# A decayed running sum behind a matmul: the last five lumps of output stored by one queue, whole

## The chip, the cores and the metric

The kernel runs on one core of a Trainium2 chip. The core has five engines that matter here: TensorE (PE: matmuls; its weight loads are listed apart as PEld), VectorE (DVE), ScalarE (ACT), GpSimd (POOL) and SyncE (SP), which computes nothing and issues transfers. Transfers between the chip's memory (HBM) and the on-chip memory (SBUF) are carried by 16 DMA engines that all queues of the core share. SyncE's queue appears in the profile as q1, GpSimd's as q0.

The metric is the device time of one execution in microseconds (us). A profile is one further execution, whose span runs from its first to its last instruction.

## The reference

```python
B, S, D = 16, 2048, 1024            # x: [B, S, D], w: [D, D], decay: [D], all float32
xw = x @ w
out[:, 0, :] = xw[:, 0, :]
for t in range(1, S):
    out[:, t, :] = decay[None, :] * out[:, t - 1, :] + xw[:, t, :]
```

So there is a matmul of 32,768 rows by 1024 x 1024, and behind it, for each of the 16 batches and each of the 1024 features, a recurrence over 2048 time steps. Input and output are 134 MB each.

## The kernel before, in words

**Tiling.** The rows are cut into 64 chunks of 512 time steps, and the chunks are taken in pairs (1024 time steps), except the last two, which are worked one at a time. A tile is 128 output features by the time steps of its pair or chunk. There are K = 8 tiles to a pair, so 31 x 8 + 2 x 8 = 264 tiles (the list `slots`). In the code `left` is the tile's number counted from the end: -264 to -1.

**The path of a tile.** The chunk of x is loaded by GpSimd's queue with a cast to bf16 (`load`), turned by VectorE in 32x32 blocks (L115) and copied into the order that the matmul wants (L123). TensorE makes the tile in PSUM (L131), features on the partitions and time along the row. The recurrence is then run by VectorE's scan: directly on PSUM (L221), or for "paired" tiles on every second time step with the square of the decay (L201), in which case ScalarE scales (L169, L183) and GpSimd adds (L196, L246) to make the other half. VectorE's transpose in 32x32 blocks (L258, in `back`) brings the result from features x time back to time x features, into an output tile `ot`. There are four output tiles, used in turn (L95).

**The stores.** R = 4 tiles in a row (4 x 128 features, half of the output's 1024 columns) share one output tile. This is a lump, and the class `Outlet` (L266) looks after it: when the fourth tile has been transposed, `store` (L274 on) issues the transfers. The 128 partitions of the output tile are four quarters of 32, and each quarter goes out by a store of its own, in the order 0, 2, 1, 3. A store writes 512-byte pieces: 32 partitions x 32 pieces (512 KB) for a pair of chunks, 32 x 16 (256 KB) for a single chunk. `Outlet` takes the queues that share the four stores (`queues`: the i-th store goes to the i-th queue in turn) and a number of pieces into which each store is cut along time (`pieces`).

**The order of the work.** The order of the instructions on each engine is written out by hand: the dictionary `agenda` lists for the first 34 tiles and the last 20 which step of which tile comes when, and every instruction is pinned to that order. A queue issues in that order too: a transfer whose data is not ready holds back everything behind it on the same engine. On GpSimd the adds stand in the same line as its store issues.

**The end.** The last four tiles (`left` -4 to -1) have no `Outlet`. Their results are turned by TensorE (L387) into four blocks of 128 time steps by 512 features, copied out of PSUM by ScalarE and VectorE in turn (L391), and stored by SyncE in four stores of 256 KB with 2 KB pieces (L393).

**What the edit touches.** For each group of four tiles the main loop makes an `Outlet` (L547). Two special cases are given there: for the four lumps whose first tile has `left` -24, -20, -16 and -12, the queues are SyncE's and GpSimd's, and for the lump with `left` -8 the stores are cut in two. All other lumps have the defaults, SyncE's queue and whole stores.

Of the kernel before, what the change touches and what calls it, by code (L numbers as in the profile page):

```python
# [25 lines left out]
def kernel(  # L26
# [26 lines left out]
    nc = tc.nc  # L53
# [12 lines left out]
    R = K // 2  # L66
# [9 lines left out]
    def ring(pool, name, count, shape, dtype=FP32):  # L76
        i = turns[name] = turns.get(name, -1) + 1
        return pool.tile(shape, dtype, name=f"{name}{i % count}")
# [46 lines left out]
    def matmul(ps, n, k, xt, t0=0, t1=TL, start=0, pairs=None):  # L125
        if pairs is None:
            rhs = xt[:, k // 2, k % 2, t0:t1]
        else:
            rhs = pairs[:, k // 2, t0 // P:t1 // P, :, k % 2].rearrange("p j i -> p (j i)")
        lhs = wsb[:, k, n].rearrange("p q i -> p (q i)")  # L130
        pin(nc.tensor.matmul(  # L131
            out=ps[:, t0:t1] if ps.shape[1] >= t1 else ps,
            lhsT=lhs,
            rhs=rhs,
            start=(k == 0 and t0 == start),
            stop=(k == K - 1),
        ))
# [376 lines left out]
    def usual(s):  # L514
        paired = [t.paired for t in tiles]
        do = [f"P{s}"] if paired[s] else []
        if paired[s - 1]:
            do.append(f"S{s - 1}")
        if not paired[s]:
            do.append(f"S{s}")  # L520
        do.append(f"C{s - 1}")
        if paired[s - 2]:
            do.append(f"B{s - 2}")
        if not paired[s - 1]:
            do.append(f"B{s - 1}")
        return do + later.get(s, []) + ["L"] * (2 if len(loads) > NQ else 1)

    def rest(s):
        do = [f"S{s - 1}"] if tiles[s - 1].paired else []
        do.append(f"C{s - 1}")  # L530
        if tiles[s - 2].paired:
            do.append(f"B{s - 2}")
        return do + [f"B{s - 1}"] + later.get(s, []) + ["L"] * len(loads)

    def perform(do):
        for deed in do:
            deeds[deed[0]](int(deed[1:] or 0))
# [3 lines left out]
    for step, (g, n) in enumerate(slots):  # L541
        T = TL * len(g)
        left = step - len(slots)
        if n % R == 0:
            ns, nj = range(n, n + R), T // P
            both = -6 * R <= left < -2 * R
            outlets = [Outlet(ns, nj, queues=(nc.sync, nc.gpsimd) if both else (nc.sync,),  # L547
                              pieces=2 if left == -2 * R else 1)]
        if left == -R:
            outlets = []  # L550
        if step == 0:
            heads = [ring(psp, "ps", 3, [128, T]) for _ in range(3)]
            firsts = [ps[:, 0:TL] for ps in heads] + [spares[0]]
            seconds = [ps[:, TL:T] for ps in heads] + [spares[1]]
            for j0, j1 in halves:
                for k in range(0, K, 2):
                    for i in range(R):
                        matmul(firsts[i], i, k, xt_of[0], j0 * P, j1 * P, pairs=xw_of[0])
            for k in range(1, K, 2):
                for i in range(R):  # L560
                    matmul(firsts[i], i, k, xt_of[0])
            for k0 in range(0, K, 2):
                for i in range(R):
                    for k in (k0, k0 + 1):
                        matmul(seconds[i], i, k, xt_of[1], 0, H * P,
                               pairs=xw_of[1] if k0 < 4 else None)
            for i in range(R):
                for k in range(K):
                    matmul(seconds[i], i, k, xt_of[1], H * P, TL, H * P,
                           pairs=xw_of[1] if i < 2 else None)  # L570
        if step < R:
            ps = heads[n] if n < 3 else tuple(spares)
        else:
            if step == K + 1:
                ps = nexts
            elif len(g) == 2 or n % R < 3:
                ps = ring(psp, "ps", 3, [128, T])
            else:
                ps = ring(psp, "spare", 1, [128, TL])
            todo = [(k, l) for k in range(K) for l in range(len(g))]  # L580
            if step < K:
                todo.sort(key=lambda kl: kl[0] % 2)
            elif step == K:
                todo = []
                nexts = ring(psp, "ps", 3, [128, T])
                for l in range(len(g)):
                    for i, both in enumerate((ps, nexts)):
                        for k in range(K):
                            matmul(both[:, l * TL:(l + 1) * TL], n + i, k, xt_of.get(g[l]),
                                   pairs=xw_of[g[l]] if g[l] in (3,) else None)  # L590
            elif step == K + 1:
                todo = []
            if left == -1:
                ps = tuple(both[:, t:t + TL // 2] for t, both in zip(
                    (0, TL // 2), (ps, ring(psp, "ps", 3, [128, TL]))))
                for t, half in zip((0, TL // 2), ps):
                    for k in range(K):
                        matmul(half, n, k, xt_of[g[0]], t, t + TL // 2, t)
                todo = []
            for k, l in todo:  # L600
                matmul(ps[:, l * TL:(l + 1) * TL], n, k, xt_of[g[l]])
        tiles.append(Tile(g, n, ps, outlets))
        do = agenda.get(step, agenda.get(left) if left >= -20 else None)
        if do is None:
            do = usual(step)
        else:
            do = do.split()
            if left == -20:
                do = rest(step) + do
        perform(do)  # L610
# [29 lines left out]
```

## Time and profile before

| what | value |
|---|---|
| runs | 908.35 us in the median of three (907.34, 908.35, 908.75) |
| profiled execution | span 907.2 us; the page gives no other time for it |
| TensorE busy | 892.8 us, 98% of the span |
| VectorE, ScalarE, GpSimd busy | 826.3, 686.2, 663.0 us |
| stores by SyncE's queue | 244 of 512 KB, 4 of 256 KB and 8 of 128 KB from `ot`, 4 of 256 KB at the end |
| stores by GpSimd's queue | 4 of 512 KB, 4 of 256 KB (5.7 us of GpSimd for the eight issues) |
| TensorE's granted clock | 0.998 of full speed |

How to read it. The time line gives, for each entry, the start and the duration in us from the start of the span, the engine (SPq is SyncE's queue), the line of the kernel, the operation, what it writes and reads, and how many were merged; in brackets stand the engine's idle time before it and what ended that. For a store, the duration is that of its issue only; the data moves afterwards, and "landing" is when the last of it has been confirmed. The table of stretches gives the length, then busy time and number of instructions of PE, PEld, DVE, ACT and POOL, then TensorE's granted clock, the mean busy share of the 16 DMA engines, and GB/s. The lines of queues give packets, MB and share of the 16 DMA engines.

### The profile page before, as it was taken

How to read it: one execution, taken by the hardware profiler on the slowest of the kernel's cores; microseconds unless marked ns; L12 is line 12 of the kernel's file. 1: busy time of each engine (PE TensorE's matmuls, PEld its weight loads, DVE VectorE, ACT ScalarE, POOL GpSimd, SP SyncE). 2: the span in 40 equal slices, each digit the busy share in tenths (PEclk: the TensorE clock that was granted, in tenths of full speed). 3: DMA queues.
4: the chain of work that ended last, by engine and by line, in shares of the span. 5: the costliest groups of instructions: out<-in, count | busy, mean ns of one | idle time of the engine just before them, and what ended most of it. 6: DMA issues, size and time to landing. Idle time of an engine off the chain costs nothing.

```text
span 907.2 us, 12004 instructions
## 1 busy us (share of the span) xinstructions
PE 892.8 (98%) x4119; PEld 411.4 (45%) x4201; DVE 826.3 (91%) x628; ACT 686.2 (76%) x955; POOL 663.0 (73%) x763
## 2 busy tenths in 40 slices
PE   9999999999999999999999999999999999999996
PEld 5444444444444444444444444444444444444443
DVE  4999989999999999899999999999999999999996
ACT  4889867777777877877877778778778778777742
POOL 7888678877777767768677777777677686776562
PEclk9999999999999999999999999999999999999999
DMA  9999999999999999999999999999999999999788
GB/s 194 194 215 220 227 215 220 215 238 255 249 250 254 241 243 259 247 244 228 227 233 227 227 232 227 226 232 233 220 230 231 228 231 223 232 229 207 153 161 211
DMA packets 397230, 204.77 MB, mean 226 GB/s; under 512 B 8816, under 2 KB 395376, under 8 KB 397168
## 3 DMA queue, kind: packets, MB, share of 16 engines
q1 hardware_dynamic: 258960, 131.62, 59.6%
q0 software_dynamic: 137920, 71.85, 58.1%
q8 instruction: 33, 0.54, 0.2%
q10 hardware_dynamic: 288, 0.52, 0.2%
q14 instruction: 29, 0.24, 0.1%
HBM read 138.42 MB, written 134.22 MB: 301 GB/s over the span
## 4 chain that ended last, share of the span: by engine, by line
PE 93%; DMA 2%; POOL 1%; issue 1%; DVE 1%; ACT 0%; POOLq 0%; DVEq 0%
PE ps L131 93%; DMA xb<-in_x_dram 2%; POOL ot L299 1%; POOL xb L105 1%; PE spare L131 1%; DVE xw L115 0%; ACT xt L123 0%; ACT xs L183 0%; DVE so L201 0%; PE spare L387 0%; DVE ot L258 0%; ACT h L169 0%; PE ps L387 0%; POOLq L635 0%; POOL xs L196 0%
## 5 line engine op out<-in xcount | busy, mean ns | idle before, releaser
L131 PE MATMUL ps<-xt,wsb 128*128 128x512 bf16 x3942 | 863.5, 378 | 4.7 <-ACT h L169 0.2
L131 PEld LDWEIGHTS <-wsb 128*128 128x128 bf16 x4152 | 405.9, 98 | 479.9 <-ACT wsb L306 0.8
L196 POOL TENSOR_TENSOR xs<-h,xs 128x512 f32<-128x512 f32 (+1 forms) x190 | 243.0, 1279 | 181.8 <-ACT h L169 79.4
L183 ACT COPY xs<-ps 128x1024 f32<-128x1024 f32 (+1 forms) x190 | 189.4, 997 | 155.3 <-PE ps L131 144.2
L258 DVE STREAM_TRANSPOSE ot<-so 128x1024 f32<-128x1024 f32 (+1 forms) x260 | 300.1, 1191 | 2.1 <-POOL so L190 1.1
L246 POOL TENSOR_TENSOR so<-h,xs 128x512 f32<-128x512 f32 (+1 forms) x190 | 241.4, 1272 | 39.0 <-ACT h L169 25.7
L123 ACT COPY xt<-xw 128x2048 bf16<-128x2048 bf16 (+1 forms) x136 | 242.3, 1790 | 7.8 <-DVE xw L115 7.6
L105 POOL DMA_DIRECT2D xb<-in_x_dram x264 | 174.3, 661 | 3.3 <-DMA ot<-in_w_dram 1.1
L169 ACT ACTIVATE h<-so,dec 128x512 f32<-128x512 f32 (+1 forms) x190 | 145.4, 766 | 27.7 <-DVE so L201 24.4
L115 DVE STREAM_TRANSPOSE xw<-xb 128x2048 f32<-128x2048 f32 (+1 forms) x78 | 147.4, 1901 | 5.5 <-DMA xb<-in_x_dram 5.5
L201 DVE TENSOR_TENSOR_SCAN so<-spare,keep,xs 128x512 f32<-128x512 f32 (+1 forms) x97 | 120.0, 1239 | 27.7 <-POOL xs L196 27.4
L201 DVE TENSOR_TENSOR_SCAN so<-spare,xs 128x512 f32<-128x512 f32 x93 | 113.3, 1220 | 27.6 <-POOL xs L196 24.6
L169 ACT ACTIVATE h<-ps,dec 128x512 f32<-128x512 f32 (+1 forms) x190 | 130.3, 686 | 0.0
L221 DVE TENSOR_TENSOR_SCAN so<-dec,ps 128x1024 f32<-128x1024 f32 x34 | 76.8, 2261 | 1.0 <-ACT h L169 1.0
L221 DVE TENSOR_TENSOR_SCAN so<-dec,keep,ps 128x1024 f32<-128x1024 f32 (+1 forms) x35 | 75.9, 2169 | 0.1
L250 ACT COPY keep<-so 128x1 f32<-128x1 f32 x136 | 25.3, 189 | 9.9 <-DVE so L221 9.4
L192 ACT COPY so<-keep 128x1 f32<-128x1 f32 x97 | 18.4, 191 | 2.6 <-DVE ot L258 2.4
L131 PE MATMUL ps<-xw,wsb 128*128 128x256 bf16 (+1 forms) x68 | 11.2, 301 | 0.1
L190 POOL MEMSET so<- 128x1 f32 x93 | 10.7, 117 | 0.6 <-DVE ot L258 0.6
L131 PE MATMUL spare<-xt,wsb 128*128 128x512 bf16 (+1 forms) x48 | 10.0, 335 | 0.0
L282 POOL DMA_DIRECT2D out_dram<-ot x8 | 5.7, 722 | 5.5 <-DVE ot L258 5.1
L299 POOL DMA_DIRECT2D ot<-in_w_dram x12 | 6.6, 546 | 3.3 <-DMA xb<-in_x_dram 2.0
(38 smaller groups left out, 44.5 us busy)
## 6 DMA issues: line engine op xcount, KB each, us to landing
out_dram<-ot SPq DMA_DIRECT2D x244, 512.0 KB, 10.9
xb<-in_x_dram POOLq DMA_DIRECT2D x248, 256.0 KB, 7.8
xb<-in_x_dram POOLq DMA_DIRECT2D x16, 128.0 KB, 5.8
out_dram<-ot POOLq DMA_DIRECT2D x4, 512.0 KB, 11.6
ot<-in_w_dram POOLq DMA_DIRECT2D x12, 128.0 KB, 5.1
out_dram<-ot SPq DMA_DIRECT2D x4, 256.0 KB
out_dram<-ot POOLq DMA_DIRECT2D x4, 256.0 KB, 8.5
out_dram<-ot SPq DMA_DIRECT2D x8, 128.0 KB, 4.3
```

The lines of the kernel that those rows point to most:

```text
L105: pin(nc.gpsimd.dma_start(out=xb_of[c][quad(q), j0:j1], in_=_ap(x, [[D, P], [P * D, j1 - j0], [1, CQ]], (b * S + t0 + j0 * P) * D + q * CQ)))
L115: pin(nc.vector.transpose(out=dst.rearrange("p (m j i) -> p j m i", m=M, i=P)[:, j0:j1, m0:m1], in_=src.rearrange("p (j m c) -> p j m c", ...
L123: pin(copy(out=xt_of[c][:, m0:m1, :, j0 * P:j1 * P], in_=src))
L131: pin(nc.tensor.matmul(out=ps[:, t0:t1] if ps.shape[1] >= t1 else ps, lhsT=lhs, rhs=rhs, start=(k == 0 and t0 == start), stop=(k == K - 1),))
L169: pin(nc.scalar.activation(out=h, in_=src, func=mybir.ActivationFunctionType.Copy, scale=dec[:, self.n:self.n + 1]))
L183: pin(nc.scalar.copy(out=self.xs, in_=self.ps))
L196: pin(nc.gpsimd.tensor_tensor(out=odds, in0=self.g, in1=odds, op=ALU.add))
L201: pin(nc.vector.tensor_tensor_scan(out=so[:, 3:T + 2:2], data0=squares[-1][:, n:n + 1].to_broadcast([128, T // 2]), data1=self.xs[:, 1:T:2 ...
L221: pin(nc.vector.tensor_tensor_scan(out=so[:, t + 2:t + 2 + size], data0=dec[:, n:n + 1].to_broadcast([128, size]), data1=ps, initial=befor ...
L246: pin(nc.gpsimd.tensor_tensor(out=self.so[:, 2:T + 2:2], in0=self.h, in1=self.xs[:, 0:T:2], op=ALU.add))
L250: pin(nc.scalar.copy(out=self.keep, in_=self.so[:, self.T + 1:self.T + 2]))
L258: pin(nc.vector.transpose(out=outlet.ot[:, :, c0:c0 + P], in_=self.so[:, 2 + t0:2 + t0 + nj * P].rearrange("p (i t) -> p i t", t=P)))
```

## The change

The two special cases are taken out. Every lump that has an `Outlet` is now stored by four whole stores on SyncE's queue.

```diff
         left = step - len(slots)
         if n % R == 0:
             ns, nj = range(n, n + R), T // P
-            both = -6 * R <= left < -2 * R
-            outlets = [Outlet(ns, nj, queues=(nc.sync, nc.gpsimd) if both else (nc.sync,),
-                              pieces=2 if left == -2 * R else 1)]
+            outlets = [Outlet(ns, nj)]
         if left == -R:
             outlets = []
```

For two lumps of 512 KB stores and two of 256 KB stores, GpSimd's queue had the second and the fourth store in the order 0, 2, 1, 3, that is quarters 2 and 3, and SyncE's had quarters 0 and 1. Now SyncE's has all four. The fifth lump, which was eight stores of 128 KB on SyncE's queue, is four of 256 KB. No instruction of TensorE, VectorE or ScalarE is added, removed or moved. GpSimd's program loses its eight store issues. SyncE's gains these eight and loses four, as the fifth lump's go from eight to four; all its stores keep their order.

## The prediction

> **What bounds the kernel now.** I read the page first, for the engine that the body hangs on:
>
> ```profile
> span 907.2 us, 12004 instructions
> PE 892.8 (98%) x4119; PEld 411.4 (45%) x4201; DVE 826.3 (91%) x628; ACT 686.2 (76%) x955; POOL 663.0 (73%) x763
> PE 93%; DMA 2%; POOL 1%; issue 1%; DVE 1%; ACT 0%; POOLq 0%; DVEq 0%
> ```
>
> TensorE is busy for 98% of the span, and its line makes 93% of the chain that ended last. The edit touches nothing before about 861 us, so only the last 46 us matter. There I followed the time line of SyncE's queue (start, duration, engine, line) together with the last copies of the other engines:
>
> ```profile
> 875.02 0.92 SPq L282 DMA_DIRECT2D out_dram<-ot  x2
> 893.73 0.32 SPq L282 DMA_DIRECT2D out_dram<-ot  x1
> 896.93 1.73 SPq L282 DMA_DIRECT2D out_dram<-ot  x1
> ...
> 897.73 0.59 ACT L391 COPY xb<-spare 128x512 f32<-128x512 f32 x1 [1.67 <-PE spare L387]
> 899.04 0.69 DVE L391 COPY h<-spare 128x512 f32<-128x512 f32 x1 [0.18 <-PE spare L387]
> ...
> 900.80 1.45 SPq L393 DMA_DIRECT2D out_dram<-xb  x3
> 902.66 0.33 SPq L393 DMA_DIRECT2D out_dram<-h  x1
> ```
>
> The first of the four final copies is done at 898.32, but its store is issued at 900.80: 2.5 us of waiting behind the eight stores of the fifth lump, which hold the queue from 893.73 to 900.70. The last copy is done at 899.73, its store leaves at 902.66, lands 3.3 us later at 906.0, and 1.2 us of closing work make the span of 907.2. So the end hangs on the stores, not on compute. Call the five lumps A (2.1 MB, first store 861.66), B (2.1 MB, 875.02), C, D and E (1.05 MB each, 880.96, 888.37, 893.73), and the last 1.05 MB, stored line by line at L393, V.
>
> Third, the table of stretches (length, busy time of each engine, clock, DMA share, GB/s):
>
> ```profile
> 849.00:852.00 3.00, 3.00 (x15) 1.37 (x14) 2.97 (x3) 1.95 (x5) 1.88 (x2) 1.00 0.97 171
> 852.00:855.00 3.00, 3.00 (x16) 1.37 (x14) 2.09 (x3) 3.00 (x5) 2.19 (x4) 1.00 1.01 217
> 855.00:858.00 3.00, 3.00 (x15) 1.37 (x14) 3.00 (x2) 1.83 (x3) 2.11 (x2) 1.00 1.02 242
> ...
> 876.00:879.00 3.00, 3.00 (x15) 1.36 (x14) 2.78 (x4) 1.76 (x7) 2.99 (x5) 1.00 0.83 160
> 879.00:882.00 3.00, 2.95 (x14) 1.36 (x14) 2.98 (x6) 1.97 (x8) 2.21 (x4) 1.00 0.83 168
> 882.00:885.00 3.00, 3.00 (x16) 1.37 (x14) 2.96 (x4) 1.09 (x5) 1.95 (x3) 1.00 1.01 207
> ...
> 898.00:900.00 2.00, 1.01 (x10) 0.77 (x8) 1.55 (x3) 0.91 (x2) 0.00 (x0) 1.00 0.55 113
> 902.00:905.00 3.00, 0.00 (x0) 0.00 (x0) 0.00 (x0) 0.00 (x0) 0.00 (x0) 0.87 0.96 357
> ```
>
> The first three rows are the lump before A, stored by SyncE alone in the row order 0, 2, 1, 3 of 32-partition quarters: it starts at 171 GB/s and reaches 242 once neighbouring stores overlap. In B, SyncE has quarters 0 and 1 only, and stays at 160 to 168. GpSimd's half of B was issued at 875.30 but moves only after SyncE's half:
>
> ```profile
> q1 hardware_dynamic: 1937, 0.98, 83.2%
> ...
> q0 software_dynamic: 285, 1.07, 90.5%
> q1 hardware_dynamic: 248, 0.12, 8.3%
> ```
>
> The first line is 876 to 882 us (q1 is SyncE's queue; packets, MB, share), the other two 882 to 888. So the two queues took turns here; they did not add up. At 898 to 900 the DMA engines are only 55% busy, at 113 GB/s, while SyncE issues E piece by piece.
>
> **The change part by part.** The profiled execution has no time on the page but its span, 907.2, which is 1.2 under the median of the three runs (908.35; they spread from 907.34 to 908.75). I work on the span and carry the difference over to the median.
>
> *Removed from GpSimd: eight store issues.* They cost 5.7 us of busy time and 5.5 us of idle time ahead of them. What is queued behind them are the adds of L196 and L246. VectorE has no wait on GpSimd after 864 us but one, of 0.22 us at 877.66, where the add stood behind B's issue. TensorE runs without a gap to 896.7. So this is worth 0 to 0.2 us; I take 0, since the last scans wait for TensorE's last columns. The rows that hide it are VectorE's, busy 5.00 us of 5 in nearly every stretch from 865 to 895.
>
> *Added to SyncE: the same eight stores, and four for E instead of eight.* Four issues of 512 KB took 5.8 us in the lump at 848.08 (0.32, 0.56, 2.14, 2.64), the later two held until earlier stores had drained. After the change A holds the queue to about 867.5, with B due at 875.02. B holds it to 880.8, and C is due at 880.96. C's four then enter as B drains, to about 885.5, before D is due at 888.37, and D's before E is due or shortly after. No lump waits long for the queue itself. E's four, at the prices of its first four now (0.32 + 1.78 + 0.97 + 1.73 and gaps, 4.98 us), would be through at 898.7, 0.4 us after V's first copy; if they find the queue drained, sooner. Freed: E's other four issues, 2.0 us, which today stand right ahead of V.
>
> *Moved: the bytes.* This is the sum. B starts moving at 875.85 (its packets begin about 0.8 us after the issue, as now), unless A is late: A alone on SyncE needs the 12.0 us of the lump at 834.27 (last landing 8.9 after its fourth issue at 837.41), so it lands at 873.7 against 875.7 now. B by the three rows above: 3 us at 171, 3 at 217, 3 at 242 is 1.89 MB, and the remaining 0.21 MB at 242 takes 0.9: drained at 885.7 (now 888). C follows without a gap and in the alternating order of quarters, so I take the warm row: 1.05 MB at 242 is 4.3 us, to 890.0. D is due before that: to 894.4. E's first packets come 0.85 after 893.73, at 894.6. Its drain is 4.3 us warm (898.9) and 4.9 us if it climbs through 171, 217 and 242 again (899.5); I take 899.5, since D has just run out. Today E drains at about 902.1, when the 2 KB packets of V take over. V's 1.05 MB at the 357 GB/s of 902 to 905 take 2.9 us: 902.4. V's last store is due at 899.73, issued by about 900.0, so it does not limit (2.6 us from issue to landing at the shortest: 902.6). From the last bytes to the landing now: 905.0 to 906.0, 1.0 us. So 903.4, and with the 1.2 us of closing 904.6: the gain is 2.6 us, 0.29%. From the median: 908.35 - 2.6 = 905.8.
>
> Nothing is newly waited for in the buffers: the four output tiles are reused in turn, so E writes over A, which lands at 873.7, long before.
>
> The page "SBUF — State Buffer" of the Trainium skill (section "Can I just issue two DMAs to hit both halves?") speaks against this: partitions 0 to 63 reach no more DMA ports than 0 to 31, and two DMAs on the two halves do not combine (it gives 6%). The first half of it the trace bears out: B's quarters 0 and 1 stay at 160 to 168 GB/s. The second it does not: the lump at 848 goes from 171 to 242, which is 42%. By that rule C to E would stay near the first rate, which is the first rival.
>
> **The rivals.**
>
> *One queue never leaves the slow rate (slower).* If stores of 512 packets in one queue keep to one half of the partitions at a time, B to E run at the 168 GB/s of 879 to 882: 5.25 MB take 31.3 us, to 907.1, then V 2.9 + 1.0 + 1.2: 912.2, 5.0 over, 913.3 in median. The point that decides is the mean rate over B to E: now it is 5.25 MB from 875.85 to 902.1, 200 GB/s; below that the kernel gets slower. At 185 it would be 910.5 in median. For it: the first 3 us of each lump. Against it: 217 and 242 right behind, in the same queue.
>
> *SyncE's issue becomes the bound (slower).* If E's four issues cost twice those of its half-sized pieces, 10 us from 893.73, V leaves at 903.7 instead of 900.80: 2.9 over, 911.3 in median. It decides from 900.7 on for E's last issue. For it: third and fourth issues of 2.1 to 2.6 us. Against it: those were twice as large, and were held by what was still to drain, and the queue at E's start holds only the end of D. The page "Perfetto Trace Analysis" of the Trainium skill (section "DMA Optimizations") has this as a rule: smaller pieces can start sooner, and where the making of descriptors limits, spreading over issuers may help. No row here separates the making of descriptors from the draining.
>
> *E starts into a drained queue and stays slow (no change).* D has drained by 894.4, so E may run all the way at the 168 to 171 of a lone store: 6.2 us, to 900.8, then V to 903.7, landing 904.7, span 905.9: gain 1.3, 907.1 in median. For it: the two SyncE stores of B never sped up. Against: they were neighbouring quarters, not alternating ones.
>
> **How the numbers follow.** A measurement of this kernel can tell about 0.2% (1.8 us) from no change; the three runs spread by 0.16%. Chances: the sum 0.55, of it 0.04 ending under 1.8 us of gain; the third rival 0.24; the slow rate 0.13; the issue 0.08. So faster 0.51, same 0.28, slower 0.21. The likeliest case has its own range: C to E at 260 GB/s would end with V's last store as the limit (902.6 + 1.2, 903.8; 904.9 in median), and at 217 GB/s C and D drain at 895.4, E at 900.2, V at 903.1, gain 1.9: 906.5. With the three runs' spread below, 904.6; the whole range reaches through the third rival and part of the slow ones, to 909.8.
>
> **What would show it.** Right: q1 alone carries bytes after 861 us; B drained by 886; rates of 217 GB/s or more from 879 to 894; V's first store issued within 0.6 us of 898.3; the last landing near 903.4. Wrong: a stretch from 882 to 894 under 200 GB/s (first rival), V's first store later than 900 with its copy long done (second), E alone at 170 GB/s between 895 and 901 (third). Also wrong would be a last copy later than 899.73, which I exclude since no compute instruction is moved.

## The result, and the profile after

The changed kernel takes 905.3 us in the median of five runs (905.08 to 905.47), against 908.35 for the kernel before. The ratio is 0.9966, with a 95% interval of 0.9954 to 0.9978: 0.34% faster, 3.0 us. The forecast was 905.8.

The page of the changed kernel says the same of the body as that of before. Only GpSimd's share has gone down, by the eight issues:

```profile
span 903.5 us, 11998 instructions
PE 892.3 (99%) x4119; PEld 411.1 (45%) x4201; DVE 825.5 (91%) x628; ACT 686.1 (76%) x955; POOL 657.2 (73%) x755
```

The span is 3.7 us shorter than that of before, as the pages round it. Of this, 0.4 us was there before the edit begins: the lump ahead of A, the same in both kernels, is issued at 847.64 instead of 848.08. What the edit did is the rest, 3.2 to 3.3 us. Where a time of the changed kernel is given "on the clock of before", these 0.44 us are added to it. The time line from E's first store on, to be laid beside the one in the prediction:

```profile
892.75 0.32 SPq L282 DMA_DIRECT2D out_dram<-ot  x1
...
897.05 0.59 ACT L391 COPY xb<-spare 128x512 f32<-128x512 f32 x1 [1.67 <-PE spare L387]
898.36 0.69 DVE L391 COPY h<-spare 128x512 f32<-128x512 f32 x1 [0.18 <-PE spare L387]
...
897.66 1.62 SPq L393 DMA_DIRECT2D out_dram<-xb  x3
899.39 0.39 SPq L393 DMA_DIRECT2D out_dram<-h  x1
```

The first final store leaves at 897.66, as soon as its copy is done (897.64); before, it stood 2.5 us behind the fifth lump. In the waits of SyncE's queue after 870 us this is to be seen as a new wait, now for ScalarE's copy and no longer for the queue (who waited for whom, us, times, longest):

```profile
SPq L393 <- ACT xb L391: 1.7, 1, 1.7
```

The table of stretches (last columns: clock, DMA share, GB/s) shows why the fifth lump was out of the way:

```profile
876.00:879.00 3.00, 3.00 (x15) 1.37 (x14) 3.00 (x5) 2.03 (x7) 1.78 (x3) 1.00 0.88 190
879.00:882.00 3.00, 2.95 (x14) 1.37 (x14) 2.97 (x5) 1.63 (x6) 0.94 (x3) 1.00 0.91 214
882.00:885.00 3.00, 3.00 (x16) 1.37 (x14) 3.00 (x5) 1.15 (x6) 1.37 (x2) 1.00 0.98 247
885.00:888.00 3.00, 3.00 (x16) 1.36 (x14) 3.00 (x6) 1.02 (x3) 1.47 (x2) 1.00 0.98 259
888.00:891.00 3.00, 2.95 (x15) 1.35 (x14) 3.00 (x4) 0.61 (x2) 0.74 (x1) 1.00 1.00 256
898.00:898.50 0.50, 0.33 (x3) 0.09 (x1) 0.32 (x2) 0.25 (x1) 0.00 (x0) 1.00 0.20 44
898.50:900.00 1.50, 0.00 (x0) 0.00 (x0) 0.56 (x1) 0.34 (x1) 0.00 (x0) 1.00 0.97 349
```

Two rows of before that the prediction does not show:

```profile
885.00:888.00 3.00, 3.00 (x16) 1.37 (x14) 3.00 (x5) 1.63 (x5) 1.33 (x2) 1.00 0.98 191
888.00:891.00 3.00, 2.95 (x15) 1.35 (x14) 3.00 (x5) 0.60 (x2) 2.12 (x4) 1.00 1.00 221
```

From 882 to 891 the one queue moves 247 to 259 GB/s, where the two queues moved 191 to 221. The stretch of 113 GB/s at 898 to 900 is gone: the mean there is now 273 GB/s, as V's stores move in it. The last two rows of the changed kernel split it up: E has all but drained at 898.0 (44 GB/s in the next half microsecond), before V's bytes begin at 898.5.

### The profile page after: what moved, and what is told of

Read it like the earlier page. It is cut to its first block, busy times and chain, and to the rows that moved or that the text cites. A ratio compares the mean times of both kernels' runs of the same rounds, so it can differ in the third digit from the quotient of the medians.

```text
span 903.5 us, 11998 instructions
## 1 busy us (share of the span) xinstructions
PE 892.3 (99%) x4119; PEld 411.1 (45%) x4201; DVE 825.5 (91%) x628; ACT 686.1 (76%) x955; POOL 657.2 (73%) x755
## 4 chain that ended last, share of the span: by engine, by line
PE 94%; DMA 1%; DVE 1%; issue 1%; POOL 1%; ACT 0%; DVEq 0%; POOLq 0%
PE ps L131 94%; DMA ot<-in_w_dram 1%; DMA xb<-in_x_dram 1%; PE spare L131 1%; POOL xb L105 1%; DVE so L221 1%; POOL ot L299 0%; DVE xw L115 0%; ACT xt L123 0%; DVE ot L258 0%; PE spare L387 0%; DVE so L201 0%; DVE wsb L306 0%; ACT xs L183 0%; PE ps L387 0%
## 5 line engine op out<-in xcount | busy, mean ns | idle before, releaser
L324 PE MATMUL spare<-idle 128*128 128x512 bf16 x22 | 6.9, 488 | 1.2 <-DVE idle L314 1.2
```

## The experiments

All ratios are to the kernel before, run on the same chip, where its median was between 908.35 and 908.92; the ratios are what compares.

| kernel | median us | ratio (95% interval) |
|---|---|---|
| changed kernel | 905.3 | 0.9966 (0.9954 to 0.9978) |
| one queue, fifth lump in pieces | 905.7 | 0.9963 (0.9950 to 0.9975) |
| two queues, fifth lump whole | 907.7 | 0.9986 (0.9977 to 0.9995) |
| one queue for A and B, fifth whole | 906.5 | 0.9978 (0.9969 to 0.9987) |
| one queue for C and D, fifth whole | 906.6 | 0.9975 (0.9964 to 0.9986) |
| one queue, neighbouring quarters | 909.2 | 1.0001 (0.9992 to 1.0010) |
| two queues, halves mixed | 907.4 | 0.9980 (0.9971 to 0.9989) |
| two queues, halves mixed, fifth whole | 906.1 | 0.9970 (0.9957 to 0.9982) |
| changed kernel, small GpSimd issues | 905.3 | 0.9961 (0.9949 to 0.9974) |
| changed kernel, fifth lump not stored | 905.8 | 0.9966 (0.9953 to 0.9978) |
| changed kernel, last store by ScalarE | 916.3 | 1.0084 (1.0070 to 1.0098) |

**Which half of the edit.** The first two kernels each make one part of it alone.

```diff
-            outlets = [Outlet(ns, nj)]
+            outlets = [Outlet(ns, nj, pieces=2 if left == -2 * R else 1)]
```

> Four lumps by SyncE's queue alone, the fifth still in eight pieces. Theory (the gain comes from bytes that drain faster when one queue takes the quarters in alternating order): the fifth lump's eight issues at 0.5 us each are through at about 897, before the first final copy at 897.6, so the time is that of the changed kernel, 3 us (0.33%) under before, within 0.6 us. Rival (the gain is that the fifth lump's issues no longer stand ahead of the final stores): the final stores leave near 900.8 as before, and the time is within 0.8 us of before.

```diff
-            outlets = [Outlet(ns, nj)]
+            both = -6 * R <= left < -2 * R
+            outlets = [Outlet(ns, nj, queues=(nc.sync, nc.gpsimd) if both else (nc.sync,))]
```

> Only the fifth lump is changed: whole stores, while the four lumps before it keep both queues. Theory (drain): the hole of 113 GB/s at 898 to 900 closes, but B to D still drain late; the fifth lump is drained at about 900.7 instead of 902.1, 1.4 us (0.15%) under before, about half of the change. Rival (issue): the whole gain of 3 us is here.

With one queue and the fifth lump still in eight pieces, the time is that of the changed kernel. The pieces cost nothing here, because the queue ahead of them is empty enough: they enter it at half a microsecond each and are through at 898.5, and the first final store, whose copy ends at 899.16, leaves at 899.18. (In the execution that was profiled everything stands 1.5 us later than in the changed kernel, from the lump ahead of A on, which is issued at 849.17.) With the fifth lump whole and two queues, a gain of 0.14% is left, as forecast: the hole at 898 to 900 closes to 209 GB/s, but the drain stays late. So the long issue of the pieces before was a consequence of the full queue, not its cause, and the pieces cost time only where the drain is late.

**Halves or queues.** This is the main question: is it that there were two queues, or which quarters each got? The third kernel keeps one queue and changes only the order of the quarters; the fourth keeps two queues and the pieces and deals the quarters otherwise.

```diff
-                for i, q in enumerate((0, 2, 1, 3)):
+                for i, q in enumerate(self.order):
...
-            outlets = [Outlet(ns, nj)]
+            late = -6 * R <= left
+            outlets = [Outlet(ns, nj, order=(0, 1, 2, 3) if late else (0, 2, 1, 3))]
```

> The changed kernel with the quarters of the last five lumps in the order 0, 1, 2, 3 instead of 0, 2, 1, 3. Theory (a store of 32 partitions uses half of what the DMA engines can read, and only neighbours from different halves add up): B to E drain at about 190 GB/s instead of 240, 27.6 us for 5.25 MB instead of 22, 5 us over the changed kernel and 2 over before (908 to 912 in all). Rival (the rate rises because more than two stores are in the queue, whatever their partitions): within 0.6 us of the changed kernel.

One queue with neighbouring quarters loses the whole gain: 909.2, level with the kernel before. Some of its stretches (the two left out have 201 and 193 GB/s):

```profile
876.00:879.00 3.00, 3.00 (x16) 1.35 (x14) 3.00 (x5) 2.21 (x8) 1.61 (x4) 1.00 0.85 176
879.00:882.00 3.00, 3.00 (x16) 1.35 (x15) 3.00 (x5) 1.44 (x7) 1.41 (x2) 1.00 0.86 173
...
888.00:891.00 3.00, 3.00 (x15) 1.34 (x14) 3.00 (x4) 0.61 (x2) 0.97 (x2) 1.00 0.95 230
```

Here the second store of B is of quarter 1 and brings nothing over the first. The right rows to lay beside these are those of a kernel with the order 0, 2, 1, 3 whose B starts at the same time. The changed kernel's B starts half a microsecond sooner (874.49 against 875.01); that of the kernel without E's stores, described further down, starts at 874.95:

```profile
876.00:879.00 3.00, 3.00 (x15) 1.37 (x14) 3.00 (x5) 2.22 (x8) 1.61 (x4) 1.00 0.85 176
879.00:882.00 3.00, 2.95 (x15) 1.37 (x14) 3.00 (x5) 1.45 (x7) 1.34 (x2) 1.00 0.93 218
```

So both start at 176 GB/s. In the next 3 us, as the second store follows the first, nothing is gained if it is quarter 1 (173), and 24% if it is quarter 2 (218). Taken by single microseconds, the order 0, 1, 2, 3 stays at 165 to 181 GB/s from 876 to 887 but for one: 245 from 882 to 883, which is where, at that rate, the bytes of quarter 1 end and those of 2 begin. From 888 on, with many stores of the smaller kind in the queue, it reaches 230 all the same. That is at least part of why the loss against the changed kernel was 0.35%, 3.2 us, and not the 5 expected.

```diff
             outlets = [Outlet(ns, nj, queues=(nc.sync, nc.gpsimd) if both else (nc.sync,),
-                              pieces=2 if left == -2 * R else 1)]
+                              pieces=2 if left == -2 * R else 1,
+                              order=(0, 1, 2, 3) if both else (0, 2, 1, 3))]
```

> The kernel before with the quarters of the four shared lumps dealt 0, 1, 2, 3, so that SyncE's queue gets quarters 0 and 2 and GpSimd's gets 1 and 3. Theory (halves): SyncE's part of A and B speeds up behind its first store from 168 towards 217 GB/s, its part of B takes 5.4 us instead of 6.2, and the end comes 0.8 to 2 us (0.1 to 0.2%) sooner than before. Rival (taking turns between two queues is itself the cost): within 0.5 us of before.

> The kernel before with quarters 0 and 2 on SyncE's queue and 1 and 3 on GpSimd's for the four shared lumps, and the fifth lump whole. Theory (what cost the time was that each queue's half came from one half of the partitions, not that there are two queues): the fifth lump is drained before 899.5 and the time is within 0.8 us of the changed kernel, 2.2 to 3 us under before. Rival (two queues take turns and lose by that): 1.3 us under before, as with the fifth lump whole alone.

The second of these is the same kernel without the line of `pieces`. Dealing the quarters so that each queue has one of either half brings 0.20% with two queues and pieces. With the fifth lump whole it brings 0.30%, and its interval covers the changed kernel's ratio. Two of its stretches, still with half of the four lumps' bytes on GpSimd's queue:

```profile
879.00:882.00 3.00, 2.95 (x14) 1.37 (x14) 3.00 (x5) 1.98 (x8) 2.28 (x4) 1.00 0.96 240
...
885.00:888.00 3.00, 3.00 (x15) 1.36 (x14) 3.00 (x5) 1.58 (x4) 1.39 (x2) 1.00 0.99 278
```

Before, these were 168 and 191. So most of what the two queues cost was not that there were two, but that each had its two stores from the same 64 partitions, while the queues' bytes went out one after the other. With the fifth lump whole, that is all that the runs can tell. With the pieces kept, two queues with mixed halves (0.9980) still stand behind one queue (0.9963); the intervals just touch. There the pieces are held again: the seventh takes 1.43 us to issue, at 897.47, and from 899 to 900 only 122 GB/s move.

**Which lumps.** With the fifth lump whole, one queue for one pair only: first for A and B, then for C and D.

```diff
-            both = -6 * R <= left < -2 * R
+            both = -4 * R <= left < -2 * R
```

> Fifth lump whole, the first two lumps (512 KB stores) by SyncE's queue alone, the third and fourth by both queues. Theory: most of the gain beyond the whole fifth lump is the second lump, drained at 885 instead of 888; 2 to 3 us under before. Rival (the third and fourth lumps, with their smaller stores, are what two queues slow): 1.3 us under before, as with the fifth lump whole alone.

```diff
-            both = -6 * R <= left < -2 * R
+            both = -6 * R <= left < -4 * R
```

> Fifth lump whole, the third and fourth lumps by SyncE's queue alone, the first two by both queues. Theory: the second lump is drained at 888 as before, the rest follows at about 245 GB/s, 3.15 MB in 12.9 us, to 901, as late as with the fifth lump whole alone: 1.0 to 2.0 us under before. Rival: the whole 3 us.

Both give about 2 us (0.22% and 0.25%), of which 0.14% is the whole fifth lump that both contain. What one queue adds to that is 0.08% for A and B and 0.11% for C and D, and with the 0.14% this makes 0.33%, about the changed kernel's 0.34%. The intervals, 0.1% to either side, are too wide to say whether the parts add up exactly. My view that most of it lay in the second lump falls. With B on two queues, C and D wait behind it in SyncE's queue, and then drain far faster than the 245 GB/s that I had put in, at 304 GB/s and in the next 3 us at 266:

```profile
888.00:891.00 3.00, 2.95 (x14) 1.37 (x14) 3.00 (x5) 0.60 (x2) 0.74 (x1) 1.00 1.08 304
```

**What bounds the end now.** The fifth lump's stores left out altogether:

```diff
-                if not outlet.missing:
+                if outlet.kept and not outlet.missing:
...
-            outlets = [Outlet(ns, nj)]
+            outlets = [Outlet(ns, nj, kept=left != -2 * R)]
```

> The changed kernel without the stores of the fifth lump, 1.05 MB that are left out of the output. Theory: in the changed kernel the fifth lump is drained at about 898.0, as the first final store's bytes begin to move, so the end now hangs on the final copies and issues, and the time falls by 0.5 us or less. Rival (the drain is still the bound): the time falls by 2 us or more, up to the 4 us that the 1.05 MB take.

Taking 1.05 MB of stores away saves nothing: 905.8, the ratio of the changed kernel. In its time line the final copies and stores stand to each other nearly as they did, all about 0.5 us later. The first and the last copy begin at 897.51 and 898.82, and their stores leave 0.61 and 1.24 us after that (0.61 and 1.03 in the changed kernel):

```profile
898.12 1.53 SPq L393 DMA_DIRECT2D out_dram<-xb  x3
900.06 0.33 SPq L393 DMA_DIRECT2D out_dram<-h  x1
```

So in the changed kernel the drain no longer sets the end; the final copies, their issues and their way to memory do.

**What GpSimd's freed time is worth.**

```diff
+                    if self.extra and i % 2:
+                        scrap = const.tile([128, 8], FP32, name="scrap", bufs=8)
+                        pin(nc.gpsimd.dma_start(
+                            out=scrap[quad(q)], in_=self.ot[quad(q), 0, c0:c0 + 8]))
```

> The changed kernel, with eight extra transfers of 1 KB from the output tile to a scrap tile issued by GpSimd at the places where its stores stood, so that GpSimd again waits for VectorE's transposes and spends its issue time. Theory: GpSimd's issues put off the fifth lump's first store by about 0.5 us against the first lump's (32.1 us between them in all kernels with these issues, 31.5 in the two without) and the last copy by 0.25 us, so the end moves by 0.2 to 0.5 us at most. Rival (a large part of the 3 us comes from the freed GpSimd): 1.5 us or more over the changed kernel.

Eight issues put back on GpSimd cost nothing that the runs can tell (905.3), and the 0.5 us by which E should have been late did not come (31.51 us from A's first store to E's). They are 0.5 us each instead of 0.65 to 0.8, and as they read only what the first tile of a lump wrote, they come sooner than the stores had: A's at 858.3, 3.5 us ahead of A's first store, where GpSimd's first store had come 0.3 us behind it. So this kernel does not bring back the delays that GpSimd's stores had made, and its test is weak. The kernel with mixed halves and the fifth lump whole says more: it has GpSimd's stores at their old places, and its time is the changed kernel's within the interval. A large share for GpSimd is out; the quarter of a microsecond that the traces show is not. From A's first store to the end of the last copy it is 38.07 us before and 38.05 with two queues for A and B, against 37.82 in the changed kernel, 37.82 with one queue for A and B, and 37.81 here. The two larger issues of B on GpSimd (875.30, 1.56 us) go with a wait of VectorE of 0.22 us at 877.66 that is gone in the changed kernel.

**A try for more.** As the end hung on the final stores' issue, the last one was given to ScalarE's queue.

```diff
-            pin(nc.sync.dma_start(
+            pin((nc.scalar if i == nb - 1 else nc.sync).dma_start(
                 out=_ap(out, [[D, 128], [1, CH]], (b * S + t0 + i * 128) * D + CH),
```

> The changed kernel with the last of the four final stores issued by ScalarE's queue, which is idle by then, instead of by SyncE's behind the third. Theory (the end now hangs on the final copies and their issues): the last store leaves at its copy's end, 0.3 us sooner, and so does the end: 0 to 0.4 us under the changed kernel, too little to be told apart by the runs. Rival (the drain still limits): no change in the last landing against the last copy.

It was 7.6 us slower than the kernel before, and so nearly 11 us slower than the changed one, for a reason that neither theory had. The waits of SyncE's queue and the time line name it:

```profile
SPq L282 <- DMA out_dram<-h: 13.2, 1, 13.2
...
886.34 15.75 SPq L282 DMA_DIRECT2D out_dram<-ot  x4
899.21 0.37 ACTq L393 DMA_DIRECT2D out_dram<-h  x1
```

SyncE's and ScalarE's transfers share eight completion semaphores, dealt out in turn when the program is built, and a store waits until the transfer that had its semaphore last has landed. The trace has the number of each transfer's semaphore: the last store got one ahead of a store of D. So D's second store, which stands long before it in the program, waited 13.2 us for that last store to land. The run says nothing on the 0.3 us that it was made for; no kernel here beats the changed one by more than its interval.

## Why the prediction was right, and which terms were off

*The end hangs on the drain of the stores (right for the kernel before).* The hidden cost was in the rate at which A to E leave, as the sum had it. The rate with alternating quarters was taken from the lump at 848 and held: 190, 214, 247 in B where the sum had 171, 217, 242, and 256 to 259 behind it instead of 242. One of the signs that it had named was missed by a hair: 214 GB/s from 879 to 882, where 217 was asked.

*E drained at 899.5 (mis-sized by about a microsecond).* It had all but drained at about 898.0, or 898.4 on the clock of before. About 0.5 us of it is that E was ready sooner against A's first store (31.52 us after it instead of 32.07), which the step on GpSimd's issues had put at nothing; the rest is the rate. The sum's 4.9 us for E's climb also hold only with steps half as long as those of the rows that it names, which it does not say; with their 3 us each it is 5.5.

*V follows at the drain's heels (did not hold).* The sum let V's bytes start as E's end and take 2.9 us. Once E was out of the way so early, V was bound by its own copies and issues, as leaving E out showed. Its bytes began half a microsecond after the drain. The last store was issued at 899.39, on the clock of before 899.8, and landed 3.2 us later, not in the 2.6 of the shortest. This is the path that the prediction had at the lower end of its range only, with V's last store as the limit; it put that at 904.9.

*The number.* On the clock of before the last landing was 903.1, against 903.4 in the sum. The closing took 0.9 us instead of 1.2; the traces of these kernels have either the one or the other, whatever the edit. So the gain in the median was 3.0 us where 2.6 were forecast. That the sum came so near owes something to luck: E was a microsecond early, and V did not follow it at once.

*GpSimd's issues are worth 0 to 0.2 us, taken as 0 (a little low).* The last copy comes 0.25 us sooner, and E's first store 0.55. The step had looked at VectorE's one wait of 0.22 us. The time lines show two more delays that are not listed as waits: before, VectorE's scan at 864.90 starts as the add behind A's issues ends (864.87), and its transposition at 879.03 as a later add ends (879.00). Counted from A's first store, VectorE was behind the changed kernel by 0.1 us at 874.92, 0.4 at 877.66 and 0.56 at 880.90. Of this, 0.25 us is left at the last copy: TensorE waited 0.22 us for GpSimd's add before its first final turning at 896.93, and in the changed kernel it does not.

*The first rival (one queue stays slow)* did not come, but its mechanism is real: the order 0, 1, 2, 3 brought it about, at 173 to 201 GB/s until 888, and cost the whole gain. The page "SBUF — State Buffer" of the Trainium skill says (section "Door 1: The DMA port swizzle (why `[64,N]` ≈ `[32,N]`)") that partitions 0 to 63 reach no more ports than 0 to 31. The trace agrees: 176 GB/s at first, then 173 as quarter 1 follows quarter 0. The same page says (section "Can I just issue two DMAs to hit both halves?") that two transfers, one from either half, measured only 6% over one. The traces do not agree: 218 GB/s once quarter 2 follows quarter 0, against 176 before, and 304 with a backlog of such stores. The measurement decides.

*The second rival (SyncE's issue)* did not come either: E's four issues took 3.2 us (892.75 to 895.93), not the 10 that it needed, and with the fifth lump in pieces, eight issues instead of four made no difference.

*The third rival (E cold and slow)*: E began in a nearly empty queue, as it said, but climbed within 2 us. By single microseconds from 893 on the rate was 173, 162, 242 and 288 GB/s; the rival needed the 168 to stay all the way.

The page "DMA: Bandwidth & Descriptors" of the Trainium skill (section "Issuing engines are not separate DMA queues") says that issuing from several engines saves issue time and nothing else. The runs bear this out: with the halves mixed and the fifth lump whole, two queues move 242 GB/s from 879 to 891 and one moves 244, and the ratios are 0.9970 and 0.9966.

## What to carry to other kernels

When a tile is stored in strips of partitions, the order of the strips is worth a look before the number of queues: let neighbours in a queue come from different halves of the 128 partitions, and check that a split over two queues doesn't undo this. A long issue on a DMA queue can be the mark of what is still to drain ahead of it; the table of stretches in GB/s, laid beside the time line, tells the two apart. At the end of a kernel, the gains of two halves of an edit need not add up: one queue alone gave 0.37%, the whole fifth lump alone 0.14%, and both together 0.34%. The pieces cost time only while the drain was late, and as soon as the drain was out of the way, the last copies and their stores were the limit.

## What the runs showed that was not expected

- Two queues with stores waiting did not share the DMA engines evenly. GpSimd's half of B, issued at 875.30, moved only from 882, when SyncE's half, issued 0.3 us earlier, was out; SyncE's part of C, issued at 880.96, then stood behind it.
- A queue with a backlog of 256 KB stores in alternating quarters reached 304 GB/s (888 to 891, C and D on one queue), against 171 in the first 3 us of a lump.
- The final store on ScalarE's queue held a store of SyncE's queue for 13.2 us through the shared completion semaphores.
- What stays open: why GpSimd's half of B waited for SyncE's to be out, while later stores of the two queues moved side by side; how much the second queue costs beyond the halves when the fifth lump is in pieces; and whether V could land sooner, since the run meant to show it was spoilt by the semaphores.
